# Hybrid decoder layer: where in its buffer a split weight begins, for the products that come out transposed

## The chip, the cores and the metric

The kernel runs on one core of one Trainium2 chip. The metric is device time in microseconds of one execution, as the median of several.

## The reference, cut to what matters

The layer works on 256 tokens of width 2048 in float32: a half step of a SwiGLU feed-forward, then two token mixers side by side (latent attention with 16 heads, and a gated linear recurrence with 16 heads), then a second half step.

```python
def swiglu(h, w_gate, w_up, w_down):
    return (jax.nn.silu(h @ w_gate) * (h @ w_up)) @ w_down
...
    for l in range(DEPTH):
        h = rmsnorm(x, ffn1_norm_pre[l])
        x = x + MACARON_SCALE * rmsnorm(swiglu(h, ffn1_w_gate[l], ffn1_w_up[l], ffn1_w_down[l]), ffn1_norm_post[l])
        h = rmsnorm(x, mix_norm_pre[l])
        y = token_mixer(h, positions, w_in[l], mla_q_norm[l], mla_w_q_up[l], mla_kv_norm[l], mla_w_kv_up[l],
                        mla_w_o[l], lb_table[l], hgrn_out_norm[l], hgrn_w_o[l], w_out[l])
        x = x + rmsnorm(y, mix_norm_post[l])
        h = rmsnorm(x, ffn2_norm_pre[l])
        x = x + MACARON_SCALE * rmsnorm(swiglu(h, ffn2_w_gate[l], ffn2_w_up[l], ffn2_w_down[l]), ffn2_norm_post[l])
```

Nearly all of the arithmetic is products of the 256 tokens with weights of 2048 x 5632, 5632 x 2048 and 2048 x 2048.

## The kernel before

A float32 number is split into two parts, a high part rounded to the matmul's input type and a low part that holds the rest. A product is then three partial ones: high by high, high by low and low by high. The operand (the tokens) is kept split in SBUF, as a tile of two halves; the weights come from HBM 512 KB at a time. `load_w` takes one such load, called a group here: a DMA on the queue of SP into `raw` (four buffers), a cast on ACT into `whi` (four buffers), a subtraction on DVE into `wlo` (four buffers). `part` gives out these two: each buffer holds 1024 + 64 elements of a partition, and a place from 0 to 63, in elements of 4 bytes, says where the 1024 begin.

Two shapes of product use the groups. `gemm_n`, called the row product here, keeps a piece of the operand in the tensor engine and streams 512 columns of weights past it, three matmuls a time (L149 to L151). `gemm_t`, the column product, keeps 128 columns of weights in the engine and streams the operand past them: the low part meets the operand's high half alone, 256 columns (L133), the high part meets both halves, 512 columns (L134). At k = 0 the high part comes first (L130, then L131). A group is eight such pairs, four values of k by two halves of the output. Column products are: gate and up of both feed-forwards except their first 512 columns (80 products of 4 groups), the projections of the gates and of the recurrence, the two output projections of the mixers (48 of 4 groups), and the attention's queries and keys in `heads_in` (16 of one group). That is 528 groups and 4224 pairs.

The places are what this document is about. `gemm_n` puts both parts at `SAME` = 32 elements. `gemm_t` asks `round()` for each group: the high part's place goes through 0, 8, ..., 56 from group to group, and the low part's through the same eight values once in eight groups, so that 64 groups in a row have all 64 combinations. In the built program the buffers of `whi` and `wlo` begin at 96 bytes modulo 256, the operands h, after, at, oa and ob at 224 and those of the attention, cqT and ckvT, at 160. An operand's rows are 1024 bytes apart and the weights' columns 512 bytes, so the distance modulo 256 between a weight and the operand that it meets is the same over a whole group. `SAME` is 128 bytes, which makes it 0 for h, after, at, oa and ob.

```python
return i % 8 * 8, i // 8 % 8 * 8
...
hi, lo = self.load_w(w[g], places=self.round())
```

The order of the work is that of the program on each engine. In the recurrence the small matmuls of its scan are laid between the groups of the column products by a plan (`tick`), in the attention between whole products.

Of the kernel before, what the change touches and what calls it, by code (L numbers as in the profile page):

```python
# [28 lines left out]
KL = LORA // P  # L29
# [17 lines left out]
SAME = 32  # L47
# [17 lines left out]
class Ops:  # L65


    def __init__(self, ctx, tc, a):
        self.tc, self.nc, self.a = tc, tc.nc, a
        self.const = ctx.enter_context(tc.tile_pool(name="const", bufs=1))  # L70
        self.wp = ctx.enter_context(tc.tile_pool(name="wp", bufs=1))
        self.small = ctx.enter_context(tc.tile_pool(name="small", bufs=3))
        self.hp = ctx.enter_context(tc.tile_pool(name="hp", bufs=1))
        self.mm = ctx.enter_context(tc.tile_pool(name="mm", bufs=2, space=PSUM))
        self.tp = ctx.enter_context(tc.tile_pool(name="tp", bufs=2, space=PSUM))
        self.sp = ctx.enter_context(tc.tile_pool(name="sp", bufs=2, space=PSUM))
        self.dram = ctx.enter_context(tc.tile_pool(name="dram", bufs=1, space=DRAM))
        self.slots = KF // 4
        self.count = 0
        self.mhalf = self.const.tile([P, 8], F32, name="mhalf")  # L80
        self.nc.vector.memset(self.mhalf, -0.5)
        self.ident = self.const.tile([P, P], F32, name="ident")
# [24 lines left out]
        nc.vector.tensor_tensor(out=lo, in0=raw, in1=hi.bitcast(F32), op=ALU.subtract)  # L107
        return hi, lo

    def round(self):  # L110

        i = self.count
        self.count += 1
        return i % 8 * 8, i // 8 % 8 * 8

    def gemm_t(self, w, act, kt, tick=None):

        nc = self.nc  # L120
        ps = self.mm.tile([P, 2, 512], F32, name="mm")
        for g in range(kt // 4):
            hi, lo = self.load_w(w[g], places=self.round())
            for i in range(4):
                k = g * 4 + i
                for j in range(2):
                    c = slice(i * 256 + j * P, i * 256 + (j + 1) * P)
                    both = act(k)
                    if k == 0:
                        nc.tensor.matmul(ps[:, j], hi[:, c], both, start=True, stop=False)  # L130
                        nc.tensor.matmul(ps[:, j, 0:T], lo[:, c], both[:, 0], start=False, stop=False)  # L131
                    else:
                        nc.tensor.matmul(ps[:, j, 0:T], lo[:, c], both[:, 0], start=False, stop=False)  # L133
                        nc.tensor.matmul(ps[:, j], hi[:, c], both, start=False, stop=k == kt - 1)  # L134
            if tick:
                tick()
        return ps
# [401 lines left out]
def mla(ops, mp, c_q, hm, h, fac, rows, oa, gate):  # L539
    nc, a, small, tp, sp, ident = ops.nc, ops.a, ops.small, ops.tp, ops.sp, ops.ident  # L540
    V, S, G = nc.vector, nc.scalar, nc.gpsimd

    def latent(ps, name, norm):
        w = ops.bcast(norm, 0)
        res = mp.tile([P, 2, KL, T], F32R, name=name)
        for tt in range(NT):
            ssq = small.tile([P, 1], F32, name="cssq")
            y = ps[tt] if isinstance(ps, list) else ps[:, tt]
            ops.square_sum(ssq, y, LORA)
            rstd = ops.rstd(ssq, fac[:, tt, 1:2])  # L550
            cn = small.tile([P, LORA], F32, name="xn", bufs=2)
            V.scalar_tensor_tensor(out=cn, in0=y, scalar=rstd, in1=w, op0=ALU.mult, op1=ALU.mult)
            ops.transposed(cn, res, 0, tt)
        return lambda k: res[:, :, k, :]
# [18 lines left out]
    cq = latent(c_q, "cqT", "mla_q_norm")  # L573
    ckv = latent(ops.gemm_n(a["w_ckv"][0], h, KD), "ckvT", "mla_kv_norm")
# [3 lines left out]
    hi, lo = ops.load_w(a["w_krope"][0], places=(0, 0))  # L578
# [38 lines left out]

    def heads_in(pair, step):
        qn = mp.tile([P, 2, T], F32, name="qn", bufs=3)
        ops.total(qn, ops.gemm_t(a["w_q_nope"][pair], cq, KL))  # L620
        step()
        kn = mp.tile([P, 2, T], F32, name="kn", bufs=3)
        ops.total(kn, ops.gemm_t(a["w_k_nope"][pair], ckv, KL))
        step()
        ps = ops.gemm_n(a["w_v"][pair], ckv, KL, n=256, place=0)
        v = mp.tile([P, NT, 256], F32, name="v", bufs=3)
        S.copy(out=v, in_=ps[:, :, 0:256])
        return pair, qn, kn, v
# [52 lines left out]
    def step():  # L681
        if later:
            later.pop(0)()

    q_rope(0)
    nxt = heads_in(0, step)
    gate(1)
    q_rope(1)
    for pair in range(8):
        cur = nxt  # L690
        if pair < 7:
            nxt = heads_in(pair + 1, step)
        else:
            step()
            gate(6)
            step()
        later += scores(*cur)
        if pair % 2 == 0:
            gate(2 + pair // 2)
# [318 lines left out]
```

## Time and profile before

| | |
|---|---|
| median of 3 runs | 2506.86 us (2506.35 to 2507.48) |
| the profiled execution's own time | 2506.64 us |
| its span, first to last instruction | 2504.7 us |
| granted clock of the tensor engine | 0.999 |
| PE matmul busy | 2486.5 us, 99% |
| DVE busy | 1544.9 us, 62% |
| ACT busy | 1210.7 us, 48% |
| DMA | 482.12 MB, 192 GB/s |

PE is the tensor engine's matmuls, PEld its loads of weights, which overlap them. In a row of the groups stand the line, the engine, the operation, what is written from what, the size and the count, then the busy time in us, the mean of one in ns, and the idle time of the engine before them with what ended it. In a row of the timeline stand the start in us from the span's start, the duration in us, and the instruction. In a row of the windows stand the stretch, its length and each engine's busy time with the count of instructions.

### The profile page before, as it was taken

To read this page: it belongs to the slowest core of one execution; us is meant where nothing else is said; L and a number is where in the kernel's file an instruction comes from. 1 tells how busy PE (TensorE), PEld (TensorE's weight loads), DVE (VectorE), ACT (ScalarE), POOL (GpSimd) and SP (SyncE) were. 2 spreads that over 40 slices of the span, in tenths; PEclk is the share of its full clock that TensorE was granted. 3 is DMA by queue.
4 is the path that set the end of the run, shared out by engine and by line. 5 is a ranking of instruction groups with operands and counts; after the bars stand their busy time and mean duration, and the time that the engine had idled before them with its cause. 6 is when DMAs were issued, how large, how long until landed. Compare 5 with 4: busy or idle time off the path is not lost.

```text
span 2504.7 us, 33918 instructions
## 1 busy us (share of the span) xinstructions
PE 2486.5 (99%) x13306; PEld 2136.1 (85%) x13306; DVE 1544.9 (62%) x1845; ACT 1210.7 (48%) x1605; POOL 82.2 (3%) x108
## 2 busy tenths in 40 slices
PE   9999999999999999999999999999999999999998
PEld 7888888888887898888888888888788888888887
DVE  6656656554466666558778876665656666564444
ACT  6444444444454566444555554445544444444433
POOL 0000000000001100000000001120000000000000
PEclk9999999999999999999999999999999999999999
DMA  8555555566685444565555555567655555555665
GB/s 302 184 190 190 186 191 187 188 194 207 202 286 181 160 136 151 187 189 185 171 167 175 169 168 172 191 225 240 223 188 190 186 192 186 189 190 194 201 201 187
DMA packets 137680, 482.12 MB, mean 192 GB/s; under 512 B 15920, under 2 KB 16432, under 8 KB 136752
## 3 DMA queue, kind: packets, MB, share of 16 engines
q1 hardware_dynamic: 137520, 479.96, 58.8%
q8 instruction: 104, 1.70, 0.3%
q14 instruction: 56, 0.46, 0.1%
HBM read 473.61 MB, written 6.29 MB: 192 GB/s over the span
## 4 chain that ended last, share of the span: by engine, by line
PE 97%; DVE 1%; POOL 1%; DMA 1%; issue 1%; ACT 0%; SPq 0%; DVEq 0%; POOLq 0%; ACTq 0%
PE mm L134 36%; PE mm L133 18%; PE mm L151 12%; PE mm L150 11%; PE mm L149 11%; PE mm L130 3%; PE mm L131 1%; PE sp L852 1%; PE sp L640 0%; PE sp L639 0%; DVE x L295 0%; PE sp L840 0%; PE tp L671 0%; DVE xn L263 0%; DVE wlo L107 0%
## 5 line engine op out<-in xcount | busy, mean ns | idle before, releaser
L107 DVE TENSOR_TENSOR wlo<-raw,whi 128x1024 fp32r<-128x1024 f32 x832 | 1031.5, 1242 | 685.3 <-ACT whi L106 679.0
L106 ACT CAST whi<-raw 128x1024 fp32r<-128x1024 f32 x832 | 872.5, 1050 | 848.5 <-PE mm L134 452.7
L134 PE MATMUL mm<-h,whi 128*128 128x512 f32 x2400 | 842.2, 394 | 0.0
L133 PE MATMUL mm<-h,wlo 128*128 128x256 f32 x2400 | 672.0, 280 | 0.0
L134 PEld LDWEIGHTS mm<-h,whi 128*128 128x128 f32 x2400 | 450.9, 188 | 101.1
L133 PEld LDWEIGHTS mm<-h,wlo 128*128 128x128 f32 x2400 | 451.2, 188 | 3.5
L134 PE MATMUL mm<-after,whi 128*128 128x512 f32 x960 | 337.8, 394 | 0.0
L133 PE MATMUL mm<-after,wlo 128*128 128x256 f32 x960 | 270.6, 282 | 0.0
L149 PE MATMUL mm<-whi,at 128*128 128x512 f32 x664 | 258.3, 389 | 0.0
L150 PE MATMUL mm<-wlo,at 128*128 128x512 f32 x664 | 258.3, 389 | 0.0
L151 PE MATMUL mm<-whi,at 128*128 128x512 f32 x664 | 258.0, 389 | 0.0
L134 PEld LDWEIGHTS mm<-after,whi 128*128 128x128 f32 x960 | 180.4, 188 | 39.3
L133 PEld LDWEIGHTS mm<-after,wlo 128*128 128x128 f32 x960 | 180.6, 188 | 1.5
L150 PEld LDWEIGHTS mm<-wlo,at 128*128 128x128 f32 x664 | 124.6, 188 | 26.0
L149 PEld LDWEIGHTS mm<-whi,at 128*128 128x128 f32 x664 | 124.6, 188 | 25.9
L151 PEld LDWEIGHTS mm<-whi,at 128*128 128x128 f32 x664 | 124.6, 188 | 25.8
L149 PE MATMUL mm<-whi,after 128*128 128x512 f32 x304 | 121.6, 400 | 0.4 <-ACT after L190 0.4
L151 PE MATMUL mm<-whi,after 128*128 128x512 f32 x304 | 118.9, 391 | 0.0
L150 PE MATMUL mm<-wlo,after 128*128 128x512 f32 x304 | 118.5, 390 | 0.0
L134 PE MATMUL mm<-ob,whi 128*128 128x512 f32 x240 | 84.3, 394 | 0.0
L134 PE MATMUL mm<-oa,whi 128*128 128x512 f32 x240 | 84.1, 393 | 0.0
L141 ACT COPY m<-mm 128x512 f32<-128x512 f32 x56 | 32.8, 587 | 95.8 <-PE mm L134 95.8
(306 smaller groups left out, 2814.0 us busy)
## 6 DMA issues: line engine op xcount, KB each, us to landing
raw<-in_ffn_w_down SPq DMA_DIRECT2D x176, 512.0 KB, 4.3
raw<-in_ffn_w_gate SPq DMA_DIRECT2D x175, 512.0 KB, 4.3
raw<-in_ffn_w_up SPq DMA_DIRECT2D x175, 512.0 KB, 4.3
raw<-in_w_ga SPq DMA_DIRECT2D x32, 512.0 KB, 3.5
raw<-in_mla_w_o SPq DMA_DIRECT2D x32, 512.0 KB, 3.8
raw<-in_w_hq SPq DMA_DIRECT2D x32, 512.0 KB, 3.7
raw<-in_w_hf SPq DMA_DIRECT2D x32, 512.0 KB, 3.5
raw<-in_w_hi SPq DMA_DIRECT2D x32, 512.0 KB, 3.5
```

The lines of the kernel that those rows point to most:

```text
L106: nc.scalar.copy(out=hi, in_=raw)
L107: nc.vector.tensor_tensor(out=lo, in0=raw, in1=hi.bitcast(F32), op=ALU.subtract)
L130: nc.tensor.matmul(ps[:, j], hi[:, c], both, start=True, stop=False)
L131: nc.tensor.matmul(ps[:, j, 0:T], lo[:, c], both[:, 0], start=False, stop=False)
L133: nc.tensor.matmul(ps[:, j, 0:T], lo[:, c], both[:, 0], start=False, stop=False)
L134: nc.tensor.matmul(ps[:, j], hi[:, c], both, start=False, stop=k == kt - 1)
L141: self.nc.scalar.copy(out=out, in_=ps[:, :, T:512])
L149: nc.tensor.matmul(o, both[:, 0, r], hi[:, c], start=k == 0, stop=False)
L150: nc.tensor.matmul(o, both[:, 0, r], lo[:, c], start=False, stop=False)
L151: nc.tensor.matmul(o, both[:, 1, r], hi[:, c], start=False, stop=k == kt - 1)
L852: nc.tensor.matmul(ps[:, 0, j], B[:, j], A[:, j], start=True, stop=True)
```

## The change

The column products no longer go round. Every group puts its low part at `place` and its high part 16 elements, 64 bytes, before it. `place` is `SAME` except in `heads_in`, where it is 16 elements less, since those operands begin 64 bytes earlier modulo 256. With that the low part begins at the same address as the operand modulo 256, and the high part 64 bytes before it, in all 528 groups. The function that went round and its counter are gone, so that lines behind it have smaller numbers. The instructions of each engine, their order, the DMAs, the tiles and the tiles' addresses are those of before. The row products and the loads that give their own places are not touched.

```diff
-    def round(self):
-
-        i = self.count
-        self.count += 1
-        return i % 8 * 8, i // 8 % 8 * 8
-
-    def gemm_t(self, w, act, kt, tick=None):
+    def gemm_t(self, w, act, kt, tick=None, place=SAME):
...
-            hi, lo = self.load_w(w[g], places=self.round())
+            hi, lo = self.load_w(w[g], places=(place - 16, place))
...
-        ops.total(qn, ops.gemm_t(a["w_q_nope"][pair], cq, KL))
+        ops.total(qn, ops.gemm_t(a["w_q_nope"][pair], cq, KL, place=SAME - 16))
...
-        ops.total(kn, ops.gemm_t(a["w_k_nope"][pair], ckv, KL))
+        ops.total(kn, ops.gemm_t(a["w_k_nope"][pair], ckv, KL, place=SAME - 16))
```

More of the change, by code (lines that the diff above doesn't have):

```diff
@@ L78, in __init__ @@
         self.slots = KF // 4
-        self.count = 0
         self.mhalf = self.const.tile([P, 8], F32, name="mhalf")
```

## The prediction

> **What bounds the kernel now.** I read the page first, for the engine on the path, then the groups, for what that engine waits for, then the timeline of the tensor engine (PE), start by start.
>
> ```profile
> span 2504.7 us, 33918 instructions
> PE 2486.5 (99%) x13306; PEld 2136.1 (85%) x13306; DVE 1544.9 (62%) x1845; ACT 1210.7 (48%) x1605; POOL 82.2 (3%) x108
> PE 97%; DVE 1%; POOL 1%; DMA 1%; issue 1%; ACT 0%; SPq 0%; DVEq 0%; POOLq 0%; ACTq 0%
> ...
> L107 DVE TENSOR_TENSOR wlo<-raw,whi 128x1024 fp32r<-128x1024 f32 x832 | 1031.5, 1242 | 685.3 <-ACT whi L106 679.0
> L106 ACT CAST whi<-raw 128x1024 fp32r<-128x1024 f32 x832 | 872.5, 1050 | 848.5 <-PE mm L134 452.7 <-PE mm L151 350.7 <-issue 16.5
> L134 PE MATMUL mm<-h,whi 128*128 128x512 f32 x2400 | 842.2, 394 | 0.0
> L133 PE MATMUL mm<-h,wlo 128*128 128x256 f32 x2400 | 672.0, 280 | 0.0
> ```
>
> PE is busy 99% of the span and is 97% of the chain. Its two big groups have 0.0 us of idle before them, while ACT, which makes whi, idles 848.5 us, nearly all of it until PE has used up an older buffer. So the weights are ready early and PE sets the end. What counts then is how far apart two starts of PE are; the "mean ns of one" holds overlap with the next matmul and is not the price of one. I call one low-part matmul (L133 or L131, 256 columns) and one high-part matmul (L134 or L130, 512 columns) a pair. The second half of the last feed-forward has the column products back to back:
>
> ```profile
> 1809.71 0.48 PE L130 MATMUL mm<-h,whi 128*128 128x512 f32 x1
> ...
> 2257.17 0.39 PE L149 MATMUL mm<-whi,at 128*128 128x512 f32 x1
> ```
>
> ```profile
> 1790.00:2262.00 472.00, 421.09 (x1200) 225.44 (x1200) 1.00 0.58 187
> ...
> 1790.00:2262.00 472.00, 29.93 (x80) 15.03 (x80) 1.00 0.58 187
> ```
>
> The first fence is the start of the first pair and of the first matmul behind the last one. The second counts high-part matmuls in that stretch, on L134 and on L130. 447.46 us over 1280 pairs is 349.6 ns a pair.
>
> **What the places do to a pair, as the trace shows it.** Going round means that this one execution has tried all 64 combinations of places, each for whole groups (one load, eight pairs). From the order of the loads and the addresses each group's distance from the operand is known. I write it as (high part, low part), in bytes modulo 256. The change uses (-64, 0). Group 34 of the column products has it, and so has one near the end:
>
> ```profile
> 147.53 0.28 PE L133 MATMUL mm<-h,wlo 128*128 128x256 f32 x1
> 147.64 0.39 PE L134 MATMUL mm<-h,whi 128*128 128x512 f32 x1
> 147.87 0.28 PE L133 MATMUL mm<-h,wlo 128*128 128x256 f32 x1
> ...
> 150.25 0.28 PE L133 MATMUL mm<-h,wlo 128*128 128x256 f32 x1
> ...
> 2128.62 0.28 PE L133 MATMUL mm<-h,wlo 128*128 128x256 f32 x1
> ...
> 2131.34 0.28 PE L133 MATMUL mm<-h,wlo 128*128 128x256 f32 x1
> ```
>
> Eight pairs take 2.72 us both times, 340.0 ns a pair. There are eight such groups in the trace, over operands h, after and oa and over two buffers of the rotation, and all eight run at that distance from the first pair on. Now other places: (-64, 64) from 192.10, (0, 0) from 153.71, (-64, -128) from 57.04, and (64, 0) from 158.61:
>
> ```profile
> 192.10 0.28 PE L133 MATMUL mm<-h,wlo 128*128 128x256 f32 x1
> ...
> 194.57 0.28 PE L133 MATMUL mm<-h,wlo 128*128 128x256 f32 x1
> ```
>
> ```profile
> 153.71 0.28 PE L133 MATMUL mm<-h,wlo 128*128 128x256 f32 x1
> ...
> 155.80 0.28 PE L133 MATMUL mm<-h,wlo 128*128 128x256 f32 x1
> ```
>
> ```profile
> 57.04 0.28 PE L133 MATMUL mm<-h,wlo 128*128 128x256 f32 x1
> ...
> 59.47 0.28 PE L133 MATMUL mm<-h,wlo 128*128 128x256 f32 x1
> ```
>
> ```profile
> 158.61 0.28 PE L133 MATMUL mm<-h,wlo 128*128 128x256 f32 x1
> ...
> 161.08 0.28 PE L133 MATMUL mm<-h,wlo 128*128 128x256 f32 x1
> ```
>
> Over seven pairs these are 2.47 us or 353 ns; over six, 2.09 us or 348 ns; over seven, 2.43 us or 347 ns; over seven, 2.47 us or 353 ns. The work is the same; only the places differ. Is 340 the end of the scale? The row products stream weights of 512 columns at distance 0 from their stationary operand:
>
> ```profile
> 560.27 0.39 PE L149 MATMUL mm<-whi,at 128*128 128x512 f32 x1
> ...
> 563.67 0.39 PE L149 MATMUL mm<-whi,at 128*128 128x512 f32 x1
> ```
>
> Fifteen of them in 3.40 us, 226.7 ns for 512 columns. In proportion 768 columns, a pair, take 340.0 ns. So at (-64, 0) the column products run at the rate of the row products, and I expect nothing below that.
>
> The Trainium skill, page "SBUF — State Buffer", section "A bandwidth-pool intuition that's wrong (but worth ruling out)", gives PE a second, independent read port for loading weights and says that contention comes only from a few structural points, none of them between PE's own two reads. By it the place of the weights would be worth nothing and the sum would be 0. The rows at 147.53 and 192.10 speak against it for this case.
>
> **The change part by part.** Nothing is added, removed or moved on any engine: before and after have the same instructions in the same order, the same DMAs, tiles and tile addresses. What changes is where inside its padded buffer a weight part begins.
>
> The pairs: how many there are says the count over the whole span, of L133 and of L131.
>
> ```profile
> 0.00:2505.00 2505.00, 1104.48 (x3936) 740.15 (x3936) 1.00 0.59 192
> ...
> 0.00:2505.00 2505.00, 80.86 (x288) 54.27 (x288) 1.00 0.59 192
> ```
>
> That is 4224 pairs. Each goes from 349.6 to 340.0 ns: 9.6 ns x 4224 = 40.5 us, all of it on the path, since PE has no idle time there to give back.
>
> The start of a product: at k = 0 the order is high, low, high, low, and then low, high. Two high parts and two low parts follow each other there, 288 pairs in 144 products, and no group at (-64, 0) shows such a start. Bounds: 340.0 ns as elsewhere, or 353 as the slowest steady rows, 288 x 13 ns = 3.7 us. I take none, since four of the six neighbourhoods there are the steady ones.
>
> The makers of weights: ACT's cast writes the high part always at one place, DVE's subtraction the low part always at another. Before, each place had its turn, and the casts lie within a narrow band.
>
> ```profile
> L106 ACT CAST whi<-raw x832: 1030/1049/1088, 10.5 to 2472.3; 128x1024 fp32r<-128x1024 f32 x167
> ```
>
> From 1030 to 1088 ns over all places, so at most 39 ns more than the median. The cover is the 848.5 us of ACT's idle time: a group gives ACT 2.72 us and asks 1.05 us of it. If the cover were gone, 528 groups x 39 ns would be 21 us. I take 0.
>
> Supply: a group of 512 KB in 2.72 us is 193 GB/s. The first of the page's slices shows 302:
>
> ```profile
> GB/s 302 184 190 190 186 191 187 188 194 207 202 286 181 160 136 151 187 189 185 171 167 175 169 168 172 191 225 240 223 188 190 186 192 186 189 190 194 201 201 187
> ```
>
> So 0 for that, too.
>
> Attention and the scan: their small matmuls stand between the pairs and use results of DVE, ACT and POOL. A PE that comes there sooner may have to wait. The waits of PE now:
>
> ```profile
> PE tp L249 <- DVE xn L552: 2.6, 3, 1.0
> PE tp L614 <- POOL xn L568: 1.4, 4, 0.7
> ```
>
> The longest is 1.0 us and most are none. 384 pairs lie around attention (16 products of 8 pairs and 8 of 32), 3.7 us of the gain; I take 0.5 us lost there, with 0 and 3.7 as ends.
>
> The sum goes against the profiled execution's own time, 2506.64 us, of which 1.94 us lie outside its span: 2506.64 - 40.5 + 0.5 = 2466.6 us. The median of the runs is 0.2 us above this execution, so **2466.8 us**, 1.6% less.
>
> **The rivals.** *A steady pace in between.* The pace depends on what came before, too. (64, 0) ran at 353 ns above, but after a break for the scan it ran so:
>
> ```profile
> 1407.18 0.28 PE L133 MATMUL mm<-after,wlo 128*128 128x256 f32 x1
> ...
> 1409.22 0.28 PE L133 MATMUL mm<-after,wlo 128*128 128x256 f32 x1
> ```
>
> Six pairs in 2.04 us, 340.0. One place with two steady paces; and all eight groups at (-64, 0) were entered from the same neighbour, (-96, 0), so they may show only one of two. If the starts of products lead into the 347 ns pace of the rows at 57.04, the gain is 2.6 ns x 4224 = 11 us: 2496 us. For it: the two paces of (64, 0). Against it: 340.0 from the first pair on in eight of eight.
>
> *Slower.* The same mechanism, into the slow pace: the product's start puts the pairs into the 353 ns of the rows at 158.61, and with no change of place inside the product nothing takes them out again. Going round leaves such a pace after eight pairs; a fixed place would keep it. The price is 3.4 ns x 4224 = 14 us: 2521 us. It decides when the slow pace holds over 9.6 / 13 = 74% of the pairs.
>
> *Only a quarter.* All eight groups at (-64, 0) held k from 8 to 11. If the row of the operand counted beyond its address modulo 256, only these would run at 340 and the rest at the mean: 10 us of gain, 2497 us. Against it: the pace is the same over the four k of a group, each 1024 bytes on.
>
> *No change.* The differences belong to something that goes with the rotation and not to the places, so that it stays: 2506.9 us. Against it: eight groups, up to 2 ms apart and over three operands, with one pace. The Trainium skill's rule on PE's second read port, cited above, would end here.
>
> **How the numbers follow.** Forecast 0.73; pace in between 0.10; a quarter 0.03; no change 0.05; slower 0.09. The forecast by itself reaches from 2464 (no loss at all, and a little of the starts' waits) to 2474 us (3.7 us for the starts and 3.7 for attention lost). The range must hold eight in ten and goes up to the pace in between: 2463 to 2496 us. A difference of 0.2%, 5 us, is about what a measurement of this kernel can tell from none. Faster by more: 0.73 + 0.10 + 0.03 = 0.86; within: 0.05; slower: 0.09.
>
> **What would show it.** In the timeline of the changed kernel pairs start 340 ns apart nearly everywhere, in the first four k of a product as in the last; the stretch of 1280 pairs takes 435 us instead of 447. The groups of L134 and L133 go from 394 and 280 ns to about 389 and 276, while L149 to L151 stay. The idle time before PE's small matmuls in attention grows by under a microsecond. A timeline with 347 or 353 ns over whole products would show a rival; paces that differ between k would show the quarter; PE idle before L133 would show that supply became the bound. The forecast is wrong if the pace of the pairs is not that of their places alone.

## The result, and the profile after

The changed kernel takes 2473.23 us, median of 4 runs (2472.45 to 2473.78), against 2506.7 us before (2506.35 to 2507.48 over 4): a ratio of 0.9866 with a 95% interval from 0.9849 to 0.9883. It is 33.5 us faster; 40.0 were forecast.

The page of the changed kernel, its head and the groups that answer to those of before. L105 is the cast, L127 and L126 are the high and low part of a column product, L142 is a row product:

```profile
span 2472.0 us, 33918 instructions
PE 2454.7 (99%) x13306; PEld 2120.3 (86%) x13306; DVE 1545.2 (63%) x1845; ACT 1213.4 (49%) x1605; POOL 82.3 (3%) x108
PE 97%; DVE 1%; POOL 1%; DMA 0%; issue 0%; ACT 0%; SPq 0%; DVEq 0%; POOLq 0%; ACTq 0%
...
L105 ACT CAST whi<-raw 128x1024 fp32r<-128x1024 f32 x832 | 872.6, 1050 | 818.1 <-PE mm L127 428.1
L127 PE MATMUL mm<-h,whi 128*128 128x512 f32 x2400 | 820.8, 389 | 0.0
L126 PE MATMUL mm<-h,wlo 128*128 128x256 f32 x2400 | 663.3, 276 | 0.0
...
L142 PE MATMUL mm<-whi,at 128*128 128x512 f32 x664 | 258.3, 389 | 0.0
```

PE is still the chain, and nothing waits in front of its products. The column products' matmuls went from 394 and 280 ns to 389 and 276, those of the row products stayed at 389, as this row of before shows:

```profile
L149 PE MATMUL mm<-whi,at 128*128 128x512 f32 x664 | 258.3, 389 | 0.0
```

ACT's cast and DVE's work take what they took, and ACT still idles for PE.

The stretch of 1280 pairs in the last feed-forward, from the timeline:

```profile
1787.81 0.48 PE L123 MATMUL mm<-h,whi 128*128 128x512 f32 x1
...
2224.45 0.39 PE L142 MATMUL mm<-whi,at 128*128 128x512 f32 x1
```

436.64 us, 341.1 ns a pair, where it was 349.6. One product from its start to the start of the next, in the same timeline:

```profile
140.83 0.40 PE L123 MATMUL mm<-h,whi 128*128 128x512 f32 x1
141.07 0.28 PE L124 MATMUL mm<-h,wlo 128*128 128x256 f32 x1
141.19 0.39 PE L123 MATMUL mm<-h,whi 128*128 128x512 f32 x1
141.41 0.28 PE L124 MATMUL mm<-h,wlo 128*128 128x256 f32 x1
141.53 0.28 PE L126 MATMUL mm<-h,wlo 128*128 128x256 f32 x1
...
141.88 0.28 PE L126 MATMUL mm<-h,wlo 128*128 128x256 f32 x1
...
151.74 0.40 PE L123 MATMUL mm<-h,whi 128*128 128x512 f32 x1
```

The first three pairs take 1.05 us, 30 ns more than three at 340 (27 ns in the records' finer times). The other 29 take 9.86 us, 340.0 ns each, through all sixteen k. A product behind a break looks different:

```profile
63.32 1.03 PE L242 MATMUL tp<-ident,xn 128*128 128x128 f32 x8
64.11 0.48 PE L123 MATMUL mm<-h,whi 128*128 128x512 f32 x1
...
65.23 0.28 PE L126 MATMUL mm<-h,wlo 128*128 128x256 f32 x1
...
75.03 0.28 PE L126 MATMUL mm<-h,wlo 128*128 128x256 f32 x1
```

After eight transposes PE runs 28 pairs in 9.80 us, 350.0 ns each, to the product's end. The next product is at 340 again. Counted over the whole trace, from one low part to the next inside a product, 3420 of 4080 distances are within 1 ns of 340; some 160 are at about 350, nearly all in ten products that follow such a break. In `heads_in`, where operand and weights both stand 64 bytes earlier, the steady pairs are at 340 or 350 as well, which speaks for the distance between the two and not for a weight's own address.

### The profile page after: what moved, and what is told of

Its sections match the earlier page's. It is cut to its first block, busy times and chain, and to the rows that moved or that the text cites. A ratio compares the mean times of both kernels' runs of the same rounds, so it can differ in the third digit from the quotient of the medians.

```text
span 2472.0 us, 33918 instructions
## 1 busy us (share of the span) xinstructions
PE 2454.7 (99%) x13306; PEld 2120.3 (86%) x13306; DVE 1545.2 (63%) x1845; ACT 1213.4 (49%) x1605; POOL 82.3 (3%) x108
## 4 chain that ended last, share of the span: by engine, by line
PE 97%; DVE 1%; POOL 1%; DMA 0%; issue 0%; ACT 0%; SPq 0%; DVEq 0%; POOLq 0%; ACTq 0%
PE mm L127 36%; PE mm L126 18%; PE mm L144 12%; PE mm L142 12%; PE mm L143 12%; PE mm L123 3%; PE mm L124 1%; PE sp L845 1%; PE sp L633 0%; PE sp L632 0%; DVE x L288 0%; PE sp L833 0%; PE tp L664 0%; PE tp L242 0%; DMA raw<-in_w_cq 0%
## 5 line engine op out<-in xcount | busy, mean ns | idle before, releaser
L105 ACT CAST whi<-raw 128x1024 fp32r<-128x1024 f32 x832 | 872.6, 1050 | 818.1 <-PE mm L127 428.1
L127 PE MATMUL mm<-h,whi 128*128 128x512 f32 x2400 | 820.8, 389 | 0.0
L126 PE MATMUL mm<-h,wlo 128*128 128x256 f32 x2400 | 663.3, 276 | 0.0
L127 PEld LDWEIGHTS mm<-h,whi 128*128 128x128 f32 x2400 | 450.5, 188 | 91.0
L126 PEld LDWEIGHTS mm<-h,wlo 128*128 128x128 f32 x2400 | 450.5, 188 | 3.3
L127 PE MATMUL mm<-after,whi 128*128 128x512 f32 x960 | 330.3, 390 | 0.0
L126 PE MATMUL mm<-after,wlo 128*128 128x256 f32 x960 | 267.4, 279 | 0.0
L142 PE MATMUL mm<-whi,at 128*128 128x512 f32 x664 | 258.3, 389 | 0.0
L127 PEld LDWEIGHTS mm<-after,whi 128*128 128x128 f32 x960 | 180.3, 188 | 35.9
L126 PEld LDWEIGHTS mm<-after,wlo 128*128 128x128 f32 x960 | 180.3, 188 | 1.4
L142 PEld LDWEIGHTS mm<-whi,at 128*128 128x128 f32 x664 | 124.6, 188 | 25.9
L142 PE MATMUL mm<-whi,after 128*128 128x512 f32 x304 | 121.6, 400 | 0.4 <-ACT after L183 0.4
L127 PE MATMUL mm<-oa,whi 128*128 128x512 f32 x240 | 82.3, 390 | 0.0
L127 PE MATMUL mm<-ob,whi 128*128 128x512 f32 x240 | 82.0, 389 | 0.0
L134 ACT COPY m<-mm 128x512 f32<-128x512 f32 x56 | 32.9, 587 | 91.9 <-PE mm L127 91.9
```

The source lines that it names most:

```text
L105: nc.scalar.copy(out=hi, in_=raw)
L134: self.nc.scalar.copy(out=out, in_=ps[:, :, T:512])
L142: nc.tensor.matmul(o, both[:, 0, r], hi[:, c], start=k == 0, stop=False)
```

## The experiments

Places are written as before: (high part, low part), distance from the operand in bytes modulo 256. Each edit is to the changed kernel.

**Half of the change, twice.** The high part fixed and the low part going round, and the other way about; `count` goes up by one for each group.

```diff
-            hi, lo = self.load_w(w[g], places=(place - 16, place))
+            hi, lo = self.load_w(w[g], places=(place - 16, self.count % 8 * 8))
```

> Half of the change: the high part fixed at -64, the low part goes through its eight places from group to group. Theory of the pair of places (both distances together make the pace): only the groups in which the low part is at 0 can run at 340, and the mean of the eight groups kinds that have the high part at -64 was 348.4 ns going round, so about 2500 us, 6 us of the 33.5. Rival (each part's place has a price of its own, and half of the gain goes with each): about 2490 us.

```diff
-            hi, lo = self.load_w(w[g], places=(place - 16, place))
+            hi, lo = self.load_w(w[g], places=(self.count % 8 * 8, place))
```

> The other half: the low part fixed at 0, the high part goes through its eight places from group to group. Theory of the pair of places: the mean of the kinds with the low part at 0 was 348.2 ns going round, so about 2500 us. Rival (each part's place has a price of its own): about 2490 us.

Measured: 2499.57 us (ratio 0.9971, 0.9959 to 0.9983) and 2500.69 us (0.9976, 0.9966 to 0.9986), beside 2506.5 before. Each half alone is worth 6 to 7 us of the 33.5, as the theory of the pair said. In the traces of the two runs the groups that are at (-64, 0) are those that run at 340: of their steady pairs, the attention's left aside, 256 of 325 and 482 of 495 are within 1 ns of it, of all others 2 and 81 of over 3000. The gain belongs to the two places together.

**The high part on the other side.** (64, 0) in place of (-64, 0).

```diff
-            hi, lo = self.load_w(w[g], places=(place - 16, place))
+            hi, lo = self.load_w(w[g], places=((place + 16) % 64, place))
```

> The high part stands 64 bytes behind the operand modulo 256 instead of 64 before it; the low part stays at 0. Places theory (a pair's pace belongs to its two distances): going round, seven of eight groups at (64, 0) ran at 353 ns, so the pairs run at 353 all through and the time is about 2507 + 3.5 ns x 4224 = 2521 us, slower than before. History theory (a place has several steady paces and what ran before chooses one): (64, 0) ran at 340 ns once, after a break, so with nothing moving any more the pairs settle at 340 and the time is within 5 us of the changed kernel, 2473 us.

Measured: 2508.34 us, ratio 1.0006 (0.9997 to 1.0015). Both expectations missed. From its timeline, within one product:

```profile
86.43 0.28 PE L126 MATMUL mm<-h,wlo 128*128 128x256 f32 x1
...
96.23 0.28 PE L126 MATMUL mm<-h,wlo 128*128 128x256 f32 x1
```

28 pairs in 9.80 us: 350.0 ns, a third pace of the same place. The count behind both expectations was off by one here: of the eight groups at (64, 0) in the trace of before six ran at 353, one at 340, and one, the only one that began a product, came to 350:

```profile
828.60 0.28 PE L133 MATMUL mm<-after,wlo 128*128 128x256 f32 x1
...
830.35 0.28 PE L133 MATMUL mm<-after,wlo 128*128 128x256 f32 x1
```

Five pairs in 1.75 us. With the place fixed every product begins there, so this one group had shown the pace that stayed.

**The same places, another start.** Again (64, 0), but with the high part first at every k, so that low and high take turns also over the joints.

```diff
-                    if k == 0:
-                        nc.tensor.matmul(ps[:, j], hi[:, c], both, start=True, stop=False)
-                        nc.tensor.matmul(ps[:, j, 0:T], lo[:, c], both[:, 0], start=False, stop=False)
-                    else:
-                        nc.tensor.matmul(ps[:, j, 0:T], lo[:, c], both[:, 0], start=False, stop=False)
-                        nc.tensor.matmul(ps[:, j], hi[:, c], both, start=False, stop=k == kt - 1)
+                    nc.tensor.matmul(ps[:, j], hi[:, c], both, start=k == 0, stop=False)
+                    nc.tensor.matmul(ps[:, j, 0:T], lo[:, c], both[:, 0], start=False, stop=k == kt - 1)
```

> Places of the run at plus 64, (64, 0), which settled at 349 and 352 ns in turn, and 2508 us; now with high first at every k. Not one place differs, only what a product starts with. History theory (the start chooses among the steady paces of a place): the pairs run at 340 ns as they once did there after a break, and the time is about 2471 us. Places theory (that pace belongs to the places): 350 ns stays, only the starts get faster, about 2505 us.

Measured: 2521.31 us (2516.41 to 2521.76), ratio 1.0055 (1.0039 to 1.0072): slower than before, and outside both expectations. Its timeline tells why (L123 is the low part here, L238 a transpose):

```profile
51.83 0.28 PE L123 MATMUL mm<-h,wlo 128*128 128x256 f32 x1
...
62.03 0.28 PE L123 MATMUL mm<-h,wlo 128*128 128x256 f32 x1
62.15 1.04 PE L238 MATMUL tp<-ident,xn 128*128 128x128 f32 x8
...
63.97 0.28 PE L123 MATMUL mm<-h,wlo 128*128 128x256 f32 x1
...
73.86 0.28 PE L123 MATMUL mm<-h,wlo 128*128 128x256 f32 x1
...
74.57 0.28 PE L123 MATMUL mm<-h,wlo 128*128 128x256 f32 x1
...
85.17 0.28 PE L123 MATMUL mm<-h,wlo 128*128 128x256 f32 x1
```

The first product runs 30 pairs in 10.20 us, 340.0 ns. Then eight transposes come between, and the next runs 28 pairs in 9.89 us and the one behind it 30 in 10.60 us, 353.2 and 353.3 ns. With nothing changed but that one interruption, the slow pace stays, product after product, since high and low now take turns without end. What an event leaves behind decides the pace, and it lasts until the next event: 106 of the 144 products run at 353.2, and in the recurrence, where the scan breaks in, the pairs go back to 340 and away from it several times. The four executions lie 5 us apart, more than those of any other kernel here.

**Three more places.** The line with the minus is that of the changed kernel; in its place stand, one for each run, (0, 0), (-64, 64) and (0, -64).

```diff
-            hi, lo = self.load_w(w[g], places=(place - 16, place))
+            hi, lo = self.load_w(w[g], places=(place, place))
...
+            hi, lo = self.load_w(w[g], places=(place - 16, (place + 16) % 64))
...
+            hi, lo = self.load_w(w[g], places=(place, place - 16))
```

> Both parts at 0, as the row products have them. If the paces that a place showed for eight pairs while going round told what it keeps (the table's theory): (0, 0) had 348.8 ns over seven groups against 349.9 over all, so about 2502 us. History theory: the table tells only one of several paces of a place, and the time may be anything from 2473 to 2521 us, with the pairs in a steady pattern that need not be that of the groups before.

> High part at -64 as in the change, low part at 64 in place of 0. The table's theory: (-64, 64) had 353.3 ns over seven groups, so about 2521 us. History theory: a pace of its own, from 2473 to 2521 us.

> The change with the parts swapped: high part at 0, low part at -64. If it only matters that the two parts stand 64 bytes apart: 2473 us. The table's theory: (0, -64) had 346.3 ns, so about 2491 us. History theory: a pace of its own.

Measured, one run of each beside 2507.34 before: 2518.05, 2497.64 and 2505.6 us. Executions of one kernel lie within 2 us of each other elsewhere, 5 us in the run above. What the table of eight-pair groups promised was 2502, 2521 and 2491: wrong three times of three, by 14 to 23 us. For (-64, 64) the timeline shows 12 pairs in 4.16 us, 346.7 ns, where its groups of before had 353:

```profile
87.82 0.28 PE L126 MATMUL mm<-h,wlo 128*128 128x256 f32 x1
...
91.98 0.28 PE L126 MATMUL mm<-h,wlo 128*128 128x256 f32 x1
```

(0, -64) has several paces in one run; three products behind each other, 27, 27 and 26 pairs:

```profile
87.73 0.28 PE L126 MATMUL mm<-h,wlo 128*128 128x256 f32 x1
...
97.21 0.28 PE L126 MATMUL mm<-h,wlo 128*128 128x256 f32 x1
...
98.95 0.28 PE L126 MATMUL mm<-h,wlo 128*128 128x256 f32 x1
...
108.31 0.28 PE L126 MATMUL mm<-h,wlo 128*128 128x256 f32 x1
...
110.06 0.27 PE L126 MATMUL mm<-h,wlo 128*128 128x256 f32 x1
...
119.16 0.27 PE L126 MATMUL mm<-h,wlo 128*128 128x256 f32 x1
```

That is 351.1, 346.7 and 350.0 ns a pair, and then the three again from the first. So the pace of a group of eight pairs, entered from a neighbour with other places, does not tell the pace that a place keeps. Nor is a group that begins a product a sure guide: all seven at (0, 0) did and came to about 347, and with the place fixed 100 of the 144 products ran at 353.0 or 353.1. And that the parts stand 64 bytes apart is not the point either: (64, 0), (0, -64) and (-64, 0) give 2508, 2506 and 2473 us.

**Who collides with whom.** Again (64, 0), low first, with one load in four.

```diff
-            hi, lo = self.load_w(w[g], places=(place - 16, place))
+            if g == 0:
+                hi, lo = self.load_w(w[g], places=((place + 16) % 64, place))
```

> Places of the run at plus 64, (64, 0), low first. Left out: of each column product's groups only the first is loaded and split, and its weights are used for all groups, so three quarters of the DMAs into raw, of ACT's casts and of DVE's subtractions for the column products are gone. Theory that PE's two own reads, of the next weights and of the operand, get into each other's way: the pairs stay at 349 and 352 ns in turn in all groups, and the time at about 2508 us. Rival (the writes of ACT, DVE or the DMAs into SBUF hold up PE's reads): the pairs get faster in the stretches without these writers, towards 340 ns, and the time falls towards 2475 us.

Measured: 2508.71 us in one run, against 2508.34 with all the loads. Ten microseconds of the first feed-forward, first with all loads, then with one in four:

```profile
75.00:85.00 10.00, 10.00 (x59) 8.80 (x58) 7.26 (x8) 4.65 (x5) 0.00 (x0) 1.00 0.59 206
```

```profile
75.00:85.00 10.00, 10.00 (x60) 8.84 (x59) 3.81 (x5) 2.07 (x3) 0.00 (x0) 1.00 0.14 52
```

The columns behind the length are busy time and count of PE, PEld, DVE, ACT and POOL, then the clock, the DMAs' share and their GB/s. DVE goes from 7.26 to 3.81 us, ACT from 4.65 to 2.07, the DMAs from 206 to 52 GB/s. The pairs keep their pace, here with one load in four (L127 is the low part):

```profile
86.96 0.28 PE L127 MATMUL mm<-h,wlo 128*128 128x256 f32 x1
...
96.76 0.28 PE L127 MATMUL mm<-h,wlo 128*128 128x256 f32 x1
```

28 pairs in 9.80 us, 350.0 ns as with all the loads. With about a half to three quarters of the writers' work gone nothing moved, so the writers do not set this pace. What is left is PE's own two reads, of the weights to be loaded and of the operand that streams; that these collide is what remains, not what a run showed by itself.

**The row products' places.** Their high part 64 bytes earlier; there the operand is loaded and the weights stream.

```diff
-                                 places=(place, place))
+                                 places=(place - 16 if place >= 16 else place, place))
```

> The changed kernel with the row products' high part 64 bytes before the operand, where both parts were at 0; there the operand is loaded and the weights stream. Theory that any two reads of PE can collide by their distance: the row products at 512 columns leave 226.7 ns for 230 or more, some 4 to 7 ns on each of the 2700 or so matmuls with weights from the shared buffers, 5 to 20 us more than 2473 us. Rival (512 columns leave room enough for any load): 226.7 ns and 2473 us.

Measured: 2495.58 us in one run, 22 us more than the changed kernel, a little over the 5 to 20 expected. Eight rounds of three matmuls, from its timeline:

```profile
550.25 0.40 PE L142 MATMUL mm<-whi,at 128*128 128x512 f32 x1
...
555.88 0.40 PE L142 MATMUL mm<-whi,at 128*128 128x512 f32 x1
```

24 matmuls in 5.63 us are 234.6 ns each, where 226.7 stood before. The places count for 512 columns as well, and the row products had a good one.

**The start of a product.** The changed kernel, (-64, 0), with the high part first at every k; the edit is that of the run with another start.

> The changed kernel with the high part first at every k and not at k = 0 alone, so that high and low take turns all through, over the joints of products too. Starts theory (two low parts behind each other at k = 0, and two high parts at the joint, cost a product about 27 ns in its first three pairs): these three pairs take 1020 ns instead of 1047, about 130 times, 3.5 us less than the changed kernel, 2469.7 us. Rival (the first pairs are slow because the product is new, whatever their order): the three pairs stay at 1047 ns and the time at 2473 us. Of the eleven products that ran at 350 ns all through after a break, the starts theory expects 340 ns if it is the two low parts that make that pace, 1.5 us more.

Measured: 2471.37 us, ratio 0.9857 (0.9841 to 0.9874): 1.9 us less than the changed kernel, not the 3.5 to 5. In the feed-forwards the products' starts lost their extra and the product behind the transposes ran at 340. But in the attention PE now waits:

```profile
863.29 0.28 PE L123 MATMUL mm<-ckvT,wlo 128*128 128x256 f32 x1
863.99 0.70 PE L660 MATMUL tp<-pT,v 128*128 128x256 f32 x2 [0.42 <-ACT pT L653]
```

The short product ends sooner, the copy of the turned scores by ACT is not ready, and PE stands for 0.42 us before `values`. The trace has three such waits, 1.2 us in all, where the changed kernel has none; the weight loads in front of them wait 2.2 us. By the starts of the products, the run goes from 2.1 us ahead of the changed kernel to 0.5 behind through the attention. So the last run leaves the attention's short products as they were:

```diff
+                    high = lambda first, last: nc.tensor.matmul(ps[:, j], hi[:, c], both, start=first, stop=last)
+                    low = lambda last: nc.tensor.matmul(ps[:, j, 0:T], lo[:, c], both[:, 0], start=False, stop=last)
+                    if kt == KD or k == 0:
+                        high(k == 0, False)
+                        low(k == kt - 1)
+                    else:
+                        low(False)
+                        high(False, k == kt - 1)
```

> High first at every k, as before this, but in the products of 16 k-steps alone; the attention's 16 short products keep low first. Theory that the gain of 5.2 us (144 starts of 27 ns and the products at 350 ns) came and 3 us of it was lost where the shorter products of the attention made PE wait for ACT's copy of the turned scores: the attention now goes as in the changed kernel, the other 128 products are faster by 3.5 us and the long products after a break by some 1 us, so about 2469 us. Rival (the 3 us were lost for another reason than the short products, such as the end of a product on its low part): 2471 to 2473 us.

Measured: 2469.29 us (2468.59 to 2469.52), ratio 0.9853 (0.9838 to 0.9867). It is as expected, 3.9 us under the changed kernel by the medians and 2.1 under the run before, and the fastest of all. The three were not measured side by side; each against its own runs of the kernel before, the gains are 33.5, 35.1 and 36.7 us. Of the 2.6 us lost in the attention some 0.7 is lost in this run too, from the start of the first product of the keys to the start of the next product; the steps at the three waits are gone. Behind the transposes and over a whole product, from its timeline:

```profile
62.72 1.04 PE L244 MATMUL tp<-ident,xn 128*128 128x128 f32 x8
...
64.53 0.28 PE L123 MATMUL mm<-h,wlo 128*128 128x256 f32 x1
...
74.39 0.28 PE L123 MATMUL mm<-h,wlo 128*128 128x256 f32 x1
...
74.50 0.39 PE L122 MATMUL mm<-h,whi 128*128 128x512 f32 x1
...
85.38 0.39 PE L122 MATMUL mm<-h,whi 128*128 128x512 f32 x1
```

29 pairs in 9.86 us right after the break, and 32 pairs from one product's start to the next's in 10.88 us: 340.0 ns, joints included.

## Why the prediction was right, and where it was off

**The bound** was right: PE's starts set the time, and no wait took their place. Supply, the casts and the clock (0.999) stayed as they were, each costed at nothing.

**The pace of a pair** was right in size: 340 ns for 3420 of the 4080 distances counted above, in every k, over all operands. The rival of a quarter falls with that, and the rival of no change too. The Trainium skill's page "SBUF — State Buffer", section "A bandwidth-pool intuition that's wrong (but worth ruling out)", gives PE a second, independent read port for loading weights. Read as the prediction read it, that the place of the weights is worth nothing, it does not hold in this case: the same matmuls take 340, 350 or 353 ns a pair at different places, and with three quarters of the column products' loads left out nothing changed. That it is the two reads that meet was not shown by a run.

**The reason for it** was only half right. The prediction read a place's pace from groups of eight pairs and took eight of eight as a sign that it lasts. By the runs a place has several steady paces; what most groups of before had shown gave the wrong time for each of the four other places that were fixed, (64, 0) among them. (-64, 0) kept the pace that its groups had, one place of five. No group at (-64, 0) had begun a product, so no row told that a product's start would lead into 340; that it did is in part luck. At (64, 0) the prediction counted two paces where the trace of before had three. The rival of a pace in between named this mechanism and priced it for the whole kernel; it is there, at 350 ns, in about 160 pairs behind breaks, 1.6 us in all. The rival on the slower side is real as well, at other places: at (64, 0) with high first one interruption put the pairs on 353 ns, 106 of 144 products ran so, and the time was 2521 us, the number that this rival had.

**The start of a product** is the mis-sized term. It was put at nothing, with 3.7 us as the far bound, "since four of the six neighbourhoods there are the steady ones". Each start costs 27 ns over three pairs at 340. Before the change, the three first pairs of the 144 products, breaks included, held 9.3 us more than 340 ns a pair would take, after it 8.8, so that they gave 0.6 us and not the 4.1 that the sum had for them. That is 3.6 us of the 7.6 that lie between the 40.5 us of the pairs' sum and the 32.9 us between the two profiled executions (2506.64 and 2473.78 us). The run with high first shows that it is the order: the extra goes when no two high or low parts stand behind each other.

**The rest of the 7.6 us**: 1.6 us in the products at 350 ns. Another 1.0 us was gone before the first column product began, which no step of the prediction spoke of:

```profile
51.45 0.40 PE L130 MATMUL mm<-h,whi 128*128 128x512 f32 x1
```

```profile
52.41 0.40 PE L123 MATMUL mm<-h,whi 128*128 128x512 f32 x1
```

The first is before, the second after; in the other runs it began between 50.9 and 51.9 us, so it moves from run to run. The last 1.4 us are mostly an average taken twice: the 349.6 ns of before had the slow starts in them, and the steady pairs between stood at 349.4, which is 0.9 us over some 3600 pairs; pairs beside breaks make the rest.

**The attention** was put at 0.5 us lost. It lost none here: by the starts of the products the lead grew through it as the pairs' own did, to 0.2 us. That was 1.8 us, not the 3.7 of the prediction, since starts and pairs at 350 lie close together there. The risk named there showed up in the next step only, when its short products got faster still: up to 0.42 us of wait on ACT's copy at a time, and 2.6 us of lead gone, 0.7 of which those waits do not explain.

## What to carry to other kernels

Where matmuls stand back to back, read their starts and not their durations, and compare the pace with the best that the same column count reaches anywhere in the trace; here 226.7 ns for 512 columns marked 340.0 for a pair before any run. A pace seen for a few matmuls under changing conditions is a hint of what is possible, not of what will last: fix the place, run it, and look at the pace after an interruption as well. And where two kinds of matmul take turns, try letting them do so over the joints too: at (-64, 0) that won 2 to 4 us, at (64, 0) it cost 13, since there it kept a slow pace going. A shorter product can also only bring forward a wait on another engine.

## What the runs showed of the hardware that was not expected

The pace of PE has memory. Within one run, with the same places, the same clock and the same order of high and low, (64, 0) ran at 340.0, 350.0 (the product from 804.4 us) and 353.3 ns a pair, each over a whole product or more, and eight transposes were enough to go from the first to the last. The fast pace is not lost in the same way everywhere: at (-64, 0) with high first PE came back to 340.0 after the same break. What the state is that lasts, in PE's queue or between its two reads, no run here tells.
